# The opening of layer 1 in a two-layer hybrid block: a third weight group among the first products, token remainders on one engine

## The chip, the cores and the metric

The kernel runs on one core of a Trainium2 chip. The metric is device time in microseconds of one execution: the median of three runs is 1145.76 us, between 1138.57 and 1148.89. The profile is of one further execution.

## The reference

The reference is a two-layer block over 1024 latent tokens of width 1024 (plus 256 context tokens in layer 0). Layer 0 mixes Fourier channels and differential attention. Layer 1, where the change lies, is a gated short convolution:

```
h = rms_norm(x, g) * (1 + scale) + shift
bg, cg, xt, g = split(h @ odd_w_in, 4)          # 1024 x 1024 times 1024 x 4096
u = cg * xt
conv = sum(conv_w[t] * up[:, t:t+n] for t in range(3))
y = (bg * conv * silu(g)) @ odd_w_out
x = x + gate * y
```

## The kernel before, in words

Features lie on the 128 partitions, tokens along the free axis in two halves of 512. Every float32 product is made of three float32r matmuls: each operand is split in a rounded part and a remainder, and high times high, high times low and low times high are added up in PSUM. The helper `part` (lines 60 to 63) makes such a pair: ScalarE casts, and VectorE or GpSimd subtracts.

The products of layer 1 are further cut by a fast 2x2 block scheme. A **group** `g` is a pair of weight tiles `a`, `b` (512 KB each, `wload`, lines 1226 to 1237), and takes seven products `p` = 1 to 7 instead of eight. Groups 0 to 15 are the input projection (an even group makes `u`, the odd one after it the gate), 16 to 19 the output projection. A product is 12 matmuls of 128x512 (`quarters`, lines 639 to 648). Its moving operand `B[p]` comes from the tokens: `B[1]` and `B[2]` from half 0 alone; 5, 6, 7, 4 and 3 need half 1, whose RMS statistics are only known when layer 0's last projection is done. Its weight operand is made by `wop` (line 1239, with `wpart`, line 615): a cast on ScalarE and a remainder on VectorE or GpSimd, and for p = 5 sums of weight tiles on GpSimd (line 625).

A product adds into a PSUM bank by `"ZXZYXYXX"[p]`: p = 1, 6, 7, 4 into X, p = 5 and 3 into Y, p = 2 into Z. A group's Z bank is written by p = 2 alone and emptied by one VectorE addition (`finish1`, line 1282, `h0 += Z`). There are three X banks, two Y banks, **one Z bank**, and two more banks in the pool `pst`. With `later=True` (line 1259) a product returns its `finish1` as a function, and the caller places it later in the program.

The order of work in the opening (lines 1459 to 1487) is written out by hand, for TensorE, VectorE, ScalarE and GpSimd alike: each takes its instructions strictly in this order. Groups 0 and 1 run their products 1 and 2, then 5, 6, 7 and so on in pairs. Between the calls stand the token operands: `scaled` (row factors times scale, on VectorE, reading the PSUM bank `ps_r` that `rows_mid` filled), `t1` to `t4` (the differences), `hi` (a cast on ScalarE, line 1431) and `lo` (the remainder, line 1435, on VectorE `V` or GpSimd `G`). After the opening only TensorE's order is by hand, and the rest is placed by a scheduler when the program is built. When product 3 of a group has its weights (`wop`, p = 3), the tiles of group g + 2 are loaded. `finish1` for p = 3 of an even group also runs the convolution (`conv`, twelve short VectorE instructions, line 1315).

Of the kernel before, what the change touches and what calls it, by code (L numbers as in the profile page):

```python
# [8 lines left out]
F32 = mybir.dt.float32  # L9
F32R = mybir.dt.float32r  # L10
# [7 lines left out]
P = 128  # L18
# [4 lines left out]
KT = 8  # L23
# [14 lines left out]
def block_kernel(tc, A):  # L38
# [20 lines left out]
    def part(src, o, eng):  # L59

        nc.scalar.copy(out=o[:, 0, :], in_=src)  # L61
        eng.tensor_tensor(out=o[:, 1, :], in0=src, in1=f32(o[:, 0, :]), op=ALU.subtract)  # L62
        return o
# [1175 lines left out]
    def wop(g, p, eng=None):  # L1239
        pool = wpools[0]  # L1240
        wpools.append(wpools.pop(0))
        wops[g, p] = wpart(g, p, raws[g], done, lambda: w2.tile([P, NB], F32, name="s1", bufs=1),
                           lambda src, e: part(src, pool.tile([P, 2, NB], F32R, name="wop", bufs=4 if pool is wp else 2), e),
                           eng)
        if p == 3:
            wload(g + 2)

    banks = {}

    def product(g, p, mid=None, later=False):  # L1250
        bank = "ZXZYXYXX"[p]
        start = p in (1, 5, 2)
        if start:
            banks[g, bank] = acc.tile([P, NB], F32, name="ps" + bank, bufs={"X": 3, "Y": 2, "Z": 1}[bank])
        quarters(banks[g, bank], wops.pop((g, p)), [(x[:, 0, :], x[:, 1, :]) for x in B[p]], start, mid)
        fin = finish1 if g < 16 else finish2
        if later:
            return lambda: fin(g, p)
        fin(g, p)
# [4 lines left out]
    def finish1(g, p):  # L1264
        ct, gated = divmod(g, 2)
        X, Y_, Z = (banks.get((g, i)) for i in "XYZ")
        if p == 1:
            if g == 1:
                us[g] = [mp.tile([P, NB], F32, name="y", tag="x1ss", bufs=2) for _ in range(2)]
            elif gated:  # L1270
                us[g] = halves(xp.tile([P, T], F32, name="y", tag="x1", bufs=KT))
            else:
                i = ct % 2
                if ubuf[i] is None:
                    ubuf[i] = at0.tile([P, T], F32, name="u", tag="v0", bufs=1) if i == 0 else \
                        xp.tile([P, T], F32, name="u", tag="x1", bufs=KT)
                us[g] = halves(ubuf[i])
        h0, h1 = us[g]
        if p == 1:
            nc.scalar.copy(out=h0, in_=X)  # L1280
        elif p == 2:
            nc.vector.tensor_tensor(out=h0, in0=h0, in1=Z, op=ALU.add)
            if gated:
                nc.scalar.activation(out=h0, in_=h0, func=AF.Silu)
        elif p == 6:
            nc.scalar.copy(out=h1, in_=X)
        elif p == 7:
            c = part22[g] = mp.tile([P, NB], F32, name="c22", tag="xr", bufs=2)
            nc.scalar.copy(out=c, in_=X)  # L1289
            nc.vector.tensor_tensor(out=c, in0=c, in1=Y_, op=ALU.add)  # L1290
        elif p == 4:
            nc.vector.tensor_tensor(out=h0, in0=h0, in1=X, op=ALU.mult)
            if gated:
                nc.vector.tensor_mul(out=h0, in0=h0, in1=vv[:, 0:NB])
        elif p == 3:

            nc.vector.tensor_tensor(out=h1, in0=h1, in1=Y_, op=ALU.add)  # L1297
            if gated:
                nc.scalar.activation(out=h1, in_=h1, func=AF.Silu)
            nc.vector.tensor_tensor(out=h1, in0=h1, in1=part22.pop(g), op=ALU.mult)  # L1300
            if gated:
                nc.vector.tensor_mul(out=h1, in0=h1, in1=vv[:, NB:T])
                ysd.append(us[g])
            else:
                conv(ct, ubuf[ct % 2])
# [69 lines left out]
    for half in range(2):  # L1375
        y0(half)
        for f in range(KT):
            if half == 0 or f < KT - 1:
                w0next()
            if half == 1 and f == KT - 2:  # L1380
                wload(0)
                wload(1)
            if pend:
                ps = pend.pop(0)
            else:
                ps = proj_feat2(W[half * KT + f], half)
# [35 lines left out]
    def scaled(k):  # L1422
        t = x1[k][1]
        V.scalar_tensor_tensor(out=t, in0=t, scalar=scm(k), in1=late["r"], op0=ALU.mult, op1=ALU.mult)
# [4 lines left out]
    def hi(p, k):  # L1429
        o = B[p][k] = hB.tile([P, 2, NB], F32R, name=f"B{p}", bufs=4)  # L1430
        nc.scalar.copy(out=o[:, 0, :], in_=x1[k + 4 * (BSRC[p] // 2)][BSRC[p] % 2])

    def lo(p, k, eng):
        o = B[p][k]
        eng.tensor_tensor(out=o[:, 1, :], in0=x1[k + 4 * (BSRC[p] // 2)][BSRC[p] % 2], in1=f32(o[:, 0, :]),  # L1435
                          op=ALU.subtract)

    def shifted(k):
        scaled(k + 4)
        t = x1[k + 4][1]  # L1440
        nc.scalar.activation(out=t, in_=t, func=AF.Identity, bias=shm(k + 4))

    def t1(k):
        less(k, x1[k][0], x1[k][1], x1[k][0])
        hi(5, k)

    def t2(k):
        V.tensor_sub(out=x1[k][0], in0=x1[k + 4][1], in1=x1[k][0])
        hi(6, k)
# [5 lines left out]
    def t4(k):  # L1455
        V.tensor_sub(out=x1[k + 4][0], in0=x1[k + 4][0], in1=x1[k][0])
# [24 lines left out]
    t4(0), t4(1), lo(4, 0, V), lo(4, 1, G), t4(2), t4(3), lo(4, 2, V), lo(4, 3, V)
    product(0, 7)
    hi(3, 0), hi(3, 1), lo(3, 0, V), lo(3, 1, G), hi(3, 2), hi(3, 3), lo(3, 2, V), lo(3, 3, G)
    product(1, 7)
    wop(2, 1)
# [127 lines left out]
```

## Time and profile before

| what | us |
|---|---|
| median of three runs | 1145.76 |
| lowest, highest | 1138.57, 1148.89 |
| the profiled execution, its time | 1145.55 |
| its span, first to last instruction | 1143.8 |
| TensorE busy in the span | 1048.7 |
| VectorE, GpSimd, ScalarE busy | 757.5, 554.8, 492.7 |
| mean granted TensorE clock | 0.971 |

All times in rows count from the span's start. PE is TensorE, DVE VectorE, ACT ScalarE, POOL GpSimd, SP the engine whose queue issues the loads. A timeline row gives start, duration, engine, line, operation, output and inputs, shapes; an x2 means two instructions merged, and in brackets stand the idle time before it and what ended it. A windows row gives, for a stretch, each engine's busy time and count, the granted TensorE clock (PEclk), and what the DMA engines moved.

### The profile page before, as it was taken

How to read it: one execution, taken by the hardware profiler on the slowest of the kernel's cores; microseconds unless marked ns; L12 is line 12 of the kernel's file. 1: busy time of each engine (PE TensorE's matmuls, PEld its weight loads, DVE VectorE, ACT ScalarE, POOL GpSimd, SP SyncE). 2: the span in 40 equal slices, each digit the busy share in tenths (PEclk: the TensorE clock that was granted, in tenths of full speed). 3: DMA queues.
4: the chain of work that ended last, by engine and by line, in shares of the span. 5: the costliest groups of instructions: out<-in, count | busy, mean ns of one | idle time of the engine just before them, and what ended most of it. 6: DMA issues, size and time to landing. Idle time of an engine off the chain costs nothing.

```text
span 1143.8 us, 14185 instructions
## 1 busy us (share of the span) xinstructions
PE 1048.7 (92%) x5118; PEld 854.2 (75%) x5118; DVE 757.5 (66%) x1039; ACT 492.7 (43%) x888; POOL 554.8 (49%) x456
## 2 busy tenths in 40 slices
PE   4989898889898989999999998899999999998598
PEld 2657686668786869989988876578888888776486
DVE  4599932885859358888882376995546655578652
ACT  4463233221334357777773353543333333343320
POOL 1258656680466315766665445564344343432331
PEclk9999999999898999999999999999999999999899
DMA  9722995533220495551103642021111111111421
GB/s 341 294 93 83 270 299 179 181 90 108 74 97 10 133 259 140 132 131 60 47 28 120 203 156 92 21 71 56 56 56 56 56 41 70 56 55 65 159 80 64
DMA packets 61382, 131.12 MB, mean 115 GB/s; under 512 B 5249, under 2 KB 30209, under 8 KB 58113
## 3 DMA queue, kind: packets, MB, share of 16 engines
q1 hardware_dynamic: 60240, 125.64, 35.0%
q0 software_dynamic: 1072, 4.59, 1.1%
q8 instruction: 40, 0.66, 0.2%
q14 instruction: 30, 0.24, 0.1%
HBM read 105.57 MB, written 24.64 MB: 114 GB/s over the span
## 4 chain that ended last, share of the span: by engine, by line
PE 52%; DVE 17%; ACT 3%; DMA 2%; issue 2%; POOL 2%; SPq 0%; ACTq 0%; DVEq 0%; POOLq 0%
PE psX L646 6%; PE psX L648 6%; PE psX L647 6%; PE ps_av L1028 5%; PE psY L646 3%; PE psY L647 3%; PE psY L648 3%; PE S L978 2%; PE S L979 2%; PE ps_t L1018 2%; DVE nm L983 2%; PE ps_feat L1081 2%; PE ps_feat L1082 2%; PE ps_feat L1083 2%; DVE arena L62 2%
## 5 line engine op out<-in xcount | busy, mean ns | idle before, releaser
L61 ACT CAST wop<-wraw 128x512 fp32r<-128x512 f32 x152 | 93.6, 621 | 131.5 <-PE psY L648 30.0
L62 POOL TENSOR_TENSOR wop<-wraw,wop 128x512 fp32r<-128x512 f32 x72 | 99.4, 1383 | 77.4 <-ACT wop L61 77.3
L285 PE MATMUL ps_tok<-whi,hlo 128*128 128x512 f32 x288 | 116.9, 406 | 5.9 <-DVE hlo L394 5.9
L284 PE MATMUL ps_tok<-whi,hhi 128*128 128x512 f32 x288 | 119.9, 416 | 2.5 <-ACT hhi L390 2.5
L286 PE MATMUL ps_tok<-wlo,hhi 128*128 128x512 f32 x288 | 115.9, 402 | 0.3 <-POOL wlo L172 0.3
L983 DVE TENSOR_REDUCE nm<-S 128x1 f32<-128x1280 f32 x64 | 95.0, 1487 | 22.5 <-PE S L979 19.5
L646 PE MATMUL psX<-B,wop 128*128 128x512 f32 x240 | 97.1, 405 | 8.7 <-ACT c L1289 4.9
L994 ACT ACTIVATE p<-S,nm 128x1280 f32<-128x1280 f32 x64 | 85.3, 1332 | 45.0 <-DVE nm L983 41.3
L647 PE MATMUL psX<-B,wop 128*128 128x512 f32 x240 | 97.0, 404 | 1.5 <-POOL B L1435 1.1
L648 PE MATMUL psX<-B,wop 128*128 128x512 f32 x240 | 97.0, 404 | 0.5 <-POOL wop L62 0.5
L625 POOL TENSOR_TENSOR s<-wraw 128x512 f32<-128x512 f32 x20 | 27.7, 1383 | 122.3 <-DMA wraw<-in_wodd_dram 117.5
L625 POOL TENSOR_TENSOR wraw<-wraw 128x512 f32<-128x512 f32 x40 | 55.6, 1398 | 47.4 <-DVE wop L62 40.0
L62 DVE TENSOR_TENSOR wop<-wraw,wop 128x512 fp32r<-128x512 f32 x80 | 68.4, 857 | 13.3 <-ACT wop L61 13.0
L1028 PE MATMUL ps_av<-v,aT 128*128 128x128 f32 x640 | 76.8, 275 | 0.0
L1028 PEld LDWEIGHTS ps_av<-v,aT 128*128 128x128 f32 x640 | 74.2, 192 | 0.2
L1005 POOL TENSOR_TENSOR p<-p,cc 128x256 f32<-128x256 f32 x32 | 40.4, 1262 | 65.8 <-DVE cc L1002 45.2
L285 PEld LDWEIGHTS ps_tok<-whi,hlo 128*128 128x128 f32 x288 | 56.2, 195 | 20.6 <-DVE hlo L394 9.6
L284 PEld LDWEIGHTS ps_tok<-whi,hhi 128*128 128x128 f32 x288 | 56.0, 194 | 16.6 <-ACT hhi L390 3.8
L646 PE MATMUL psY<-B,wop 128*128 128x512 f32 x160 | 63.8, 399 | 4.8 <-DVE y L1297 3.0
L286 PEld LDWEIGHTS ps_tok<-wlo,hhi 128*128 128x128 f32 x288 | 56.1, 195 | 12.7 <-POOL wlo L172 0.7
L647 PE MATMUL psY<-B,wop 128*128 128x512 f32 x160 | 63.9, 399 | 0.3 <-POOL B L1435 0.3
L648 PE MATMUL psY<-B,wop 128*128 128x512 f32 x160 | 63.8, 399 | 0.0
(343 smaller groups left out, 2739.6 us busy)
## 6 DMA issues: line engine op xcount, KB each, us to landing
ada_raw<-in_ada_dram SPq DMA_DIRECT2D x24, 1024.0 KB, 7.4
wraw<-in_wodd_dram SPq DMA_DIRECT2D x32, 512.0 KB, 3.5
wraw<-in_wo_dram SPq DMA_DIRECT2D x24, 512.0 KB, 4.0
wraw<-in_wtok_dram SPq DMA_DIRECT2D x16, 512.0 KB, 5.1
arena<-kd SPq DMA_DIRECT2D x16, 320.0 KB, 9.1
kq<-kd SPq DMA_DIRECT2D x16, 320.0 KB, 9.8
xt<-in_xT_dram SPq DMA_DIRECT2D x16, 256.0 KB, 6.0
xr<-in_xT_dram SPq DMA_DIRECT2D x16, 256.0 KB, 4.0
```

Source lines behind the costliest of these rows:

```text
L61: nc.scalar.copy(out=o[:, 0, :], in_=src)
L62: eng.tensor_tensor(out=o[:, 1, :], in0=src, in1=f32(o[:, 0, :]), op=ALU.subtract)
L284: nc.tensor.matmul(ps, lhsT=hh, rhs=whi, start=k == 0, stop=False)
L285: nc.tensor.matmul(ps, lhsT=hl, rhs=whi, start=False, stop=False)
L286: nc.tensor.matmul(ps, lhsT=hh, rhs=wlo, start=False, stop=k == KT - 1)
L625: tt = lambda out, x, y, op: nc.gpsimd.tensor_tensor(out=out, in0=x, in1=y, op=op)
L646: nc.tensor.matmul(ps, lhsT=a, rhs=x[k][0], start=start and k == 0, stop=False, skip_group_check=not start)
L647: nc.tensor.matmul(ps, lhsT=a, rhs=x[k][1], start=False, stop=False, skip_group_check=not start)
L648: nc.tensor.matmul(ps, lhsT=b, rhs=x[k][0], start=False, stop=k == 3, skip_group_check=not start)
L983: nc.vector.tensor_reduce(out=nm, in_=S[m][:, :NKEY], op=ALU.max, axis=AX.X, negate=True)
L994: nc.scalar.activation(out=p, in_=S[m][:, :NKEY], func=AF.Exp, bias=tiles.pop((i, m, "nm")), accum_out=z)
L1028: nc.tensor.matmul(ps, lhsT=groups[i, k // 4][:, (k % 4) * P:(k % 4 + 1) * P], rhs=v[:, k * P:(k + 1) * P], start=k == 0, stop=k == NK - 1)
```

## The change

Three things are changed in the opening.

1. A third group joins it. `wload_early` loads the two weight tiles of group 2 a second time, in buffers of the tag `B3`, which the token operand `B[3]` takes over later; `wop_early` makes the operands of products 1, 2 and 5 of group 2 from them. The products (2,1) and (2,2) stand behind (1,2), and (2,5) behind (1,5), its Y bank out of the pool `pst`. Their `finish1` calls are put off (`fin2`). Later group 2's tiles come again by the usual `wload(2)`, and `wmix` redoes on GpSimd the sums that product 5 would have left in them.
2. The token remainders `lo` are all on VectorE (9 of 20 were on GpSimd), and the weight remainders of products 6, 7, 4 and 3 of groups 0 and 1 on GpSimd.
3. The order is new: `ps_r` is made in product (1,2) instead of (1,1); products 4 and 3 of group 1 and 6 of group 2 belong to the hand-written part; the multiplication of the gate of group 1 with `vv[:, 0:NB]` moves from p = 4 to p = 3.

```diff
+    def wload_early():
+        for i in range(2):
+            t = hB.tile([P, KT * P], F32, name="wraw", tag="B3", bufs=4)
+            nc.sync.dma_start(out=t, in_=A["wodd"][1, (1, 2)[i]])
+            early.append(t)
+    def wop_early(p):
+        pool = wpools[0]
+        wpools.append(wpools.pop(0))
+        wops[2, p] = wpart(2, p, early, set(), lambda: w2.tile([P, NB], F32, name="s1", bufs=1),
+                           lambda src, e: part(src, pool.tile([P, 2, NB], F32R, name="wop", bufs=4 if pool is wp else 2), e))
+    def wmix(g):
+        a, b = raws[g]
+        lo, hi = hsl
+        t = w2.tile([P, NB], F32, name="s1", bufs=1)
+        for o, x, y, op in ((t, b[:, lo], b[:, hi], ALU.add), (b[:, lo], b[:, lo], a[:, lo], ALU.subtract),
+                            (a[:, lo], t, a[:, lo], ALU.subtract), (a[:, hi], a[:, hi], a[:, lo], ALU.subtract)):
+            nc.gpsimd.tensor_tensor(out=o, in0=x, in1=y, op=op)
...
-            banks[g, bank] = acc.tile([P, NB], F32, name="ps" + bank, bufs={"X": 3, "Y": 2, "Z": 1}[bank])
+            banks[g, bank] = pst.tile([P, NB], F32, name="psY", tag="t", bufs=2) if (g, p) == (2, 5) else \
+                acc.tile([P, NB], F32, name="ps" + bank, bufs={"X": 3, "Y": 2, "Z": 1}[bank])
...
+    wload_early()
     product(0, 1)
-    wop(0, 6)
     product(0, 2, (2, stats_mid))
-    wop(1, 6, G)
-    product(1, 1, (2, rows_mid))
-    scaled(0), scaled(1), t1(0), scaled(2), t1(1), lo(5, 0, V), lo(5, 1, G), scaled(3), t1(2), t1(3), lo(5, 2, V)
-    lo(5, 3, G)
-    fin12 = product(1, 2, later=True)
-    product(0, 5)
+    wop_early(1)
+    product(1, 1)
+    wop_early(2)
+    fin12 = product(1, 2, (2, rows_mid), later=True)
+    scaled(0), scaled(1), t1(0), scaled(2), t1(1), lo(5, 0, V), lo(5, 1, V)
+    wop_early(5)
+    scaled(3), t1(2), t1(3), lo(5, 2, V), lo(5, 3, V)
+    fin2 = [product(2, p, later=True) for p in (1, 2)]
+    wop(0, 6, G)
+    product(0, 5)
+    shifted(0), shifted(1), t2(0), shifted(2), t2(1), lo(6, 0, V), lo(6, 1, V), shifted(3), t2(2), t2(3), lo(6, 2, V)
+    lo(6, 3, V)
+    wop(1, 6, G)
     product(1, 5)
...
+    product(2, 5)
+    fin12()
...
     product(0, 4)
+    wop(1, 3, G)
+    product(1, 4)
+    for f in fin2:
+        f()
+    wmix(2)
     product(0, 3)
+    wop(2, 6, V)
+    done.update(((2, 1), (2, 2), (2, 5)))
+    product(1, 3)
```

**TensorE, where the products without half-1 tokens end.** `arena_2059` and `arena_2060` are `B[1]` and `B[2]`; `B_6181` and `B_6185` are quarters of `B[5]`. Before, (1,2) is followed by (0,5):

```order
L648 MATMUL psZ<-arena_2060,wop 128x512
L646 MATMUL psY<-B_6181,wop 128x512 [waits Activation_49]
L647 MATMUL psY<-B_6181,wop 128x512 [waits DVE_49]
L648 MATMUL psY<-B_6181,wop 128x512
L646 MATMUL psY<-B_6185,wop 128x512 [waits Activation_49]
L647 MATMUL psY<-B_6185,wop 128x512 [waits Pool_49]
```

Now the last matmuls of (2,1), the first of (2,2), and further down the first of (0,5) (`B_6198` is now the first quarter of `B[5]`):

```order
L647 MATMUL psX<-arena_2059,wop 128x512
L648 MATMUL psX<-arena_2059,wop 128x512
L646 MATMUL psZ<-arena_2060,wop 128x512 [waits DVE_49,Activation_49]
L647 MATMUL psZ<-arena_2060,wop 128x512
L648 MATMUL psZ<-arena_2060,wop 128x512
L646 MATMUL psY<-B_6198,wop 128x512 [waits Activation_49]
```

The first matmul of (2,2) waits for ScalarE, which casts its weights, and for VectorE. What VectorE has to reach is its addition of (1,2)'s Z bank, since (2,2) takes the same bank.

**VectorE, where that addition stands.** Before, after the differences and the VectorE share of the remainders of `B[6]` (`B_6254` is one):

```order
L1448 TENSOR_TENSOR x_5567<-x_5727,x_5567 128x512 [waits Activation_49,Pool_49]
L1435 TENSOR_TENSOR B_6254<-x_5527,B_6254 128x512 [waits Activation_49]
L1282 TENSOR_TENSOR y<-y,psZ 128x512 [waits PE_49]
L1427 SCALAR_TENSOR_TENSOR x_5498<-x_5498,shift_90,x_5607 128x512
L1427 SCALAR_TENSOR_TENSOR x_5512<-x_5512,shift_90,x_5647 128x512
```

Now (the line numbers of the changed file are higher; L1478 was L1448, L1465 was L1435, L1308 was L1282):

```order
L1478 TENSOR_TENSOR x_5567<-x_5727,x_5567 128x512 [waits Activation_49]
L1465 TENSOR_TENSOR B_6281<-x_5527,B_6281 128x512 [waits Activation_49]
L1465 TENSOR_TENSOR B_6284<-x_5567,B_6284 128x512 [waits Activation_49]
L1308 TENSOR_TENSOR y<-y,psZ 128x512 [waits PE_49]
L1457 SCALAR_TENSOR_TENSOR x_5498<-x_5498,shift_90,x_5607 128x512
```

The addition has kept its place behind all of `B[5]` and `B[6]`: 20 instructions stand between the first `scaled` and it before, and 25 now, the five more being four remainders and one weight remainder of (2,5).

**VectorE, around the convolution of group 0.** Before, the weight remainder of (2,6) (the L62 row) stands after the fifth of the convolution's twelve instructions (L1315):

```order
L1315 SCALAR_TENSOR_TENSOR vv<-u,small,vv 128x254 [waits DVE_49]
L1315 SCALAR_TENSOR_TENSOR vv<-u,small,vv 128x255 [waits Activation_49]
L62 TENSOR_TENSOR wop<-wraw,wop 128x512 [waits Activation_49]
L1292 TENSOR_TENSOR y<-y,psX 128x512 [waits PE_49]
L1315 SCALAR_TENSOR_TENSOR vv<-u,small,vv 128x255 [waits DVE_49]
```

Now the end of the convolution (L1343, as L1315 is now called), and behind it the weight remainder of (2,6):

```order
L1343 SCALAR_TENSOR_TENSOR vv<-u,small,vv 128x254 [waits DVE_49]
L1343 SCALAR_TENSOR_TENSOR vv<-u,small,vv 128x2
L1343 SCALAR_TENSOR_TENSOR vv<-u,small,vv 128x2 [waits DVE_49] x2
L1343 SCALAR_TENSOR_TENSOR vv<-u,small,vv 128x2
L62 TENSOR_TENSOR wop<-wraw,wop 128x512 [waits DMAHW3_49,Activation_49]
L1323 TENSOR_TENSOR y<-y,psY 128x512 [waits PE_49]
```

The remainder of (2,6) is now behind the whole convolution; (2,6) itself is the product right behind (1,3) on TensorE.

More of the change, by code (lines that the diff above doesn't have):

```diff
@@ L1246, in wop @@
             wload(g + 2)
+    def wload_early():
[15 more added lines that the diff above has]
+            nc.gpsimd.tensor_tensor(out=o, in0=x, in1=y, op=op)
+    early = []
     banks = {}
@@ L1266, in finish1 @@
         X, Y_, Z = (banks.get((g, i)) for i in "XYZ")
+        if p == 5:
+            return
         if p == 1:
@@ L1292, in finish1 @@
             nc.vector.tensor_tensor(out=h0, in0=h0, in1=X, op=ALU.mult)
-            if gated:
+            if gated and g > 1:
                 nc.vector.tensor_mul(out=h0, in0=h0, in1=vv[:, 0:NB])
@@ L1301, in finish1 @@
             if gated:
+                if g == 1:
+                    nc.vector.tensor_mul(out=h0, in0=h0, in1=vv[:, 0:NB])
                 nc.vector.tensor_mul(out=h1, in0=h1, in1=vv[:, NB:T])
@@ L1362, in finish2 @@
             take(Y_, 1, (f, 1))
-    order = [(0, 1), (0, 2), (1, 1), (1, 2), (0, 5), (1, 5), (0, 6), (1, 6), (0, 7), (1, 7), (0, 4), (0, 3)]
-    for g in range(2, 14):
+    order = [(0, 1), (0, 2), (1, 1), (1, 2), (2, 1), (2, 2), (0, 5), (1, 5), (2, 5), (0, 6), (1, 6), (0, 7), (1, 7),
+             (0, 4), (1, 4), (0, 3), (1, 3), (2, 6), (2, 7)]
+    NMAN = 17
+    for g in range(3, 14):
         order += [(g, 1), (g - 1, 4), (g, 5), (g - 1, 3), (g, 6), (g, 2), (g, 7)]
@@ L1387, in block_kernel @@
             if half == 1 and f == KT - 1:
-                for q in order[:5]:
+                for q in (*order[:4], (0, 5)):
                     wop(*q)
@@ L1459, in block_kernel @@
     nc.scalar.activation(out=l2[:, 0:1], in_=ones[:, 0:1], func=AF.Silu)
+    wload_early()
     product(0, 1)
-    wop(0, 6)
     product(0, 2, (2, stats_mid))
-    wop(1, 6, G)
-    product(1, 1, (2, rows_mid))
-    scaled(0), scaled(1), t1(0), scaled(2), t1(1), lo(5, 0, V), lo(5, 1, G), scaled(3), t1(2), t1(3), lo(5, 2, V)
-    lo(5, 3, G)
-    fin12 = product(1, 2, later=True)
-    product(0, 5)
+    wop_early(1)
[10 more added lines that the diff above has]
+    lo(6, 3, V)
+    wop(1, 6, G)
     product(1, 5)
-    shifted(0), shifted(1), t2(0), shifted(2), t2(1), lo(6, 0, V), lo(6, 1, G), shifted(3), t2(2), t2(3), lo(6, 2, V)
-    lo(6, 3, G)
+    product(2, 5)
+    fin12()
     wop(0, 7, G)
-    fin12()
-    t3(0), t3(1), lo(7, 0, V), lo(7, 1, G)
+    t3(0), t3(1), lo(7, 0, V), t3(2), lo(7, 1, V), t3(3), lo(7, 2, V), lo(7, 3, V)
     product(0, 6)
-    t3(2), t3(3), lo(7, 2, V), lo(7, 3, G)
     wop(1, 7, G)
     product(1, 6)
+    t4(0), t4(1), lo(4, 0, V), t4(2), lo(4, 1, V), t4(3), lo(4, 2, V), lo(4, 3, V)
     wop(0, 4, G)
+    product(0, 7)
+    wop(1, 4, G)
+    product(1, 7)
+    hi(3, 0), hi(3, 1), lo(3, 0, V), hi(3, 2), lo(3, 1, V), hi(3, 3), lo(3, 2, V), lo(3, 3, V)
     wop(0, 3, G)
[L1481 to L1485, printed above, removed]
-    product(0, 4)
+    product(0, 4)
+    wop(1, 3, G)
[3 more added lines that the diff above has]
+    wmix(2)
     product(0, 3)
+    wop(2, 6, V)
+    done.update(((2, 1), (2, 2), (2, 5)))
+    product(1, 3)
     man.__exit__(None, None, None)
@@ L1494, in block_kernel @@
              (16, 1): [(7, 3, 4), (4, 0, 2)], (16, 5): [(4, 2, 4)], (17, 1): [(3, 0, 4)]}
-    wn = 13
+    wn = NMAN + 1
     for n, (g, p) in enumerate(order):
-        if n < 12:
+        if n < NMAN:
             continue
```

## The prediction

> **What bounds the kernel now.** I read the page's busy line first, then stretches of the windows view around the opening, then TensorE's waits there.
>
> ```profile
> PE 1048.7 (92%) x5118; PEld 854.2 (75%) x5118; DVE 757.5 (66%) x1039; ACT 492.7 (43%) x888; POOL 554.8 (49%) x456
> ```
> ```profile
> 709.90:716.70 6.80, 5.85 (x12) 3.95 (x13) 4.92 (x8) 1.18 (x3) 0.34 (x1) 0.50 0.01 2
> 716.70:744.00 27.30, 22.03 (x84) 14.69 (x83) 26.68 (x29) 16.43 (x29) 16.91 (x11) 1.00 0.09 26
> 744.00:747.40 3.40, 3.40 (x9) 2.63 (x8) 3.40 (x4) 3.00 (x6) 2.89 (x2) 0.50 0.25 102
> 774.80:992.70 217.90, 217.90 (x935) 175.06 (x934) 122.10 (x192) 79.60 (x134) 92.95 (x68) 1.00 0.17 56
> ```
>
> From 774.8 to 992.7 us TensorE is never idle and the clock is at 1.00: 217.90 busy of 217.90. So nothing else sets the pace there, and what the opening gains or loses is carried to the end one for one. Between 716.7 and 744.0 VectorE is busy for 26.68 of 27.30 us and TensorE is not: there VectorE is the bound. The stalls themselves:
>
> ```profile
> PE ps_r L228 <- DVE dg L220: 3.5, 1, 3.5
> PE psX L646 <- ACT c L1289: 2.5, 1, 2.5
> PE psX L646 <- ACT u L1286: 2.5, 1, 2.5
> PE psX L647 <- POOL B L1435: 1.1, 2, 0.8
> ```
> ```profile
> 698.43 0.40 PE L646 MATMUL psX<-arena,wop 128*128 128x512 f32 x1
> ...
> 702.63 0.28 PE L209 MATMUL ps_ss<-ones,x1ss 128*128 128x1 f32 x2
> ...
> 704.34 0.48 PE L646 MATMUL psZ<-arena,wop 128*128 128x512 f32 x1
> ...
> 706.99 0.39 PE L648 MATMUL psX<-arena,wop 128*128 128x512 f32 x1
> 710.85 2.08 PE L228 MATMUL ps_r<-dg,ones 128*128 128x512 f32 x2 [3.47 <-DVE dg L220]
> 711.93 1.42 PE L646 MATMUL psX<-arena,wop 128*128 128x512 f32 x1
> ...
> 744.01 0.63 PE L648 MATMUL psX<-B,wop 128*128 128x512 f32 x1
> ...
> 816.56 0.40 PE L646 MATMUL psX<-B,wop 128*128 128x512 f32 x1
> ```
>
> At full clock a matmul takes 217.90 / 935 = 0.233 us, so a product of twelve 2.80; at clock 0.50, from the row at 744.00, 3.40 / 8 = 0.43. The first product starts at 698.43 and the 35th at 816.56: 118.1 us for 34 products (95.2) and the token sums (702.63 to 704.34, 1.7). The opening therefore **loses 21.2 us now**: the wait for `ps_r`, its own 2.08, three stretches at half clock (a full one of 3.4 us costs 3.4 x (1 - 0.233/0.43) = 1.55), two ScalarE waits of 2.5, and small waits for remainders. That is all the change can win.
>
> **The change part by part.** Matmuls are neither added nor removed. I rebuild the same ledger of 34 products.
>
> *The early loads.* Two tiles of 512 KB more.
>
> ```profile
> wraw<-in_wodd_dram SPq DMA_DIRECT2D x32, 512.0 KB, 3.5
> 693.81 7.21 SPq L1175 DMA_DIRECT2D x1d<-x  x2
> ```
>
> SP's queue issues them behind the first of these two writes, from about 694.2, the second when the last projection has left its buffer; 3.5 us each, so they land by about 701, and the first is used at 705. Behind them only the last `x1d` write is passed, which is read at the very end. Cost 0; if they came 3 us late, (2,1) still would not wait, because of what follows.
>
> *The first wait for the Z bank.* (1,2) may start once VectorE has added (0,2)'s bank, an instruction that stands behind `dg`.
>
> ```profile
> 706.00 1.29 POOL L625 TENSOR_TENSOR wraw<-wraw 128x512 f32<-128x512 f32 x1
> 707.76 0.15 DVE L216 TENSOR_SCALAR rs<-ps_ss 128x4 f32<-128x4 f32 x1
> 707.99 1.02 POOL L218 TENSOR_TENSOR rs<-rs,mhalf 128x4 f32<-128x4 f32 x1 [0.70 <-DVE rs L216]
> 709.04 1.75 DVE L220 TENSOR_TENSOR dg<-cst,rs 128x512 f32<-128x512 f32 x1 [1.13 <-POOL rs L218]
> 710.71 0.67 DVE L1282 TENSOR_TENSOR u<-u,psZ 128x512 f32<-128x512 f32 x1
> ```
>
> The weight remainder that kept VectorE's `rs` until 707.8 is gone, so GpSimd's `rs` follows its mixing at 707.3, `dg` comes at 708.3, and the addition ends at 710.7 if `dg` again takes 1.75, at 709.7 if it takes 0.7. TensorE has finished (0,1), (0,2), the token sums and (1,1) at 698.4 + 8.4 + 1.7 = 708.5: it loses **2.1** (bounds 1.0 and 2.1). Then `ps_r` in mid-product costs **1.0**, half of 2.08 as no long idle precedes it (up to 2.1). `ps_r` is ready at 713.2, not earlier than now.
>
> *The second wait for the Z bank.* (1,2) ends at 714.5 and (2,1) at 717.3. (2,2) needs the only Z bank, which VectorE empties by an instruction behind all of `B[5]` and `B[6]`.
>
> ```profile
> 712.96 1.41 DVE L1424 SCALAR_TENSOR_TENSOR x<-x,sc,ps_r 128x512 f32<-128x512 f32 x2 [1.57 <-PE ps_r L228]
> 727.73 0.68 DVE L1282 TENSOR_TENSOR y<-y,psZ 128x512 f32<-128x512 f32 x1
> ```
> ```profile
> L1435 DVE TENSOR_TENSOR B<-x,B x11: 678/693/1772, 716.7 to 746.3; 128x512 fp32r<-128x512 f32 x11
> 738.79 3.46 DVE L1456 TENSOR_TENSOR x<-x,x 128x512 f32<-128x512 f32 x2
> 736.58 5.12 POOL L62 TENSOR_TENSOR wop<-wraw,wop 128x512 fp32r<-128x512 f32 x3
> ```
>
> Now 20 instructions take from 712.96 to 727.73, 14.8 us. The change has 25, the five more at some 0.6 each in a dense row (3.0), from 713.2: the addition runs at about 731.0 less 0.4, as GpSimd now crosses this stretch three times and not four, and ends at 731.3. TensorE stands still from 717.3 to 731.3: **14.0**. The 738.79 rows show what a crossing is: two VectorE subtractions take 3.46 us, not 1.3, while GpSimd works through the row at 736.58. So the lower bound is 25 x 0.65 with no crossing and an early `dg` (11), the upper one three more crossings (16). `B[5]` and `B[6]` are all there by then, so the small waits of now vanish in this one.
>
> *Half clock after it.* Now a 3.5 us wait was followed by two windows of 0.50 (709.90 to 716.70), a 2.5 us wait by one. For a 14 us wait I take 1.5 windows, **2.3** (1.5 to 3.1).
>
> The Trainium skill, TensorE: Matmul & The Clock Gate, Part 1, says that one busy window of about 3.4 us brings the full clock back. The rows at 709.90 show two; by the page alone both half-clock terms here would be 1.55, and the time 1158.1.
>
> *Products from then on.* From 731.3 run (2,2), (0,5), (1,5), (2,5), (0,6), (1,6), (0,7), (1,7), (0,4), (1,4), (0,3), (1,3): 33.6 us, and 2.3 for the clock, to 767.2. VectorE's remaining 12 differences and remainders of `B[7]`, `B[4]`, `B[3]`, at 0.6 to 1.3, have 8.4 us to get ahead of (0,7), since ScalarE lets `B[7]` start only when (1,5) is done; I see no wait, and the pairing hides the copies that cost 2.5 now. This is the gain of the change, and it cannot be more than the 21.2.
>
> *(2,6) behind the convolution.* Its weight remainder stands behind the whole convolution of group 0, which starts when (0,3) is done.
>
> ```profile
> 754.34 0.68 DVE L1300 TENSOR_TENSOR u<-u,c 128x512 f32<-128x512 f32 x1
> ...
> 758.21 0.69 DVE L62 TENSOR_TENSOR wop<-wraw,wop 128x512 fp32r<-128x512 f32 x1
> ...
> 767.62 0.69 DVE L1294 TENSOR_TENSOR y<-y,vv 128x512 f32<-128x512 f32 x1
> ```
>
> Now (2,6)'s remainder comes at 758.21, 3.9 us after `u*c`, and the convolution ends at 767.6, 13.3 us after it, with GpSimd crossing. In the change (0,3) ends at 764.4, `u*c` starts at 765.1, and 13.3 + 0.7 later, at 779.1, the remainder is there. TensorE has finished (1,3) at 767.2 and can run two matmuls of (2,6): 11.4, and one more for GpSimd, which is denser here (the repeated sums of `wmix`, the weights of groups 2 and 3): **12.4**. Upper bound 15. Lower bound: the reloaded tile itself. It is issued when (0,3)'s weight remainder is done, about 760, lands 3.5 us later, is mixed by three GpSimd sums of 1.3 to 1.7 and cast (0.6) by 769; with the remainder right behind the cast, (2,6) would wait 3. I take the row of the convolution, since the order is fixed.
>
> Half clock again, **2.0** (0 to 3.1), and (2,7), now directly behind (2,6) on the same X bank, waits for ScalarE's copy, **1.0** (0.5 to 1.2; the same wait now was 2.5 with ScalarE late).
>
> Sum: 2.1 + 1.0 + 14.0 + 2.3 + 12.4 + 2.0 + 1.0 = 34.8, against 21.2: **13.6 us more**. On the profiled execution's 1145.55 (span 1143.8 and 1.75 around it) this is 1159.2; its time is within 0.2 of the median. All lower ends together (1.0, 1.0, 11, 1.5, 3, 0, 0.5: 18) give 1142.4, all upper ends (2.1, 2.1, 16, 3.1, 15, 3.1, 1.2: 42.6) 1167.
>
> **The rivals.** *The third group fills the hole (not slower).* If (2,2) does not wait for VectorE, TensorE has 5.6 us more work while `B[5]` is made, the losses shrink to `ps_r`, one window and some 2 us of remainders, about 5, and the time is 1145.6 - 16 = 1129.5. For it: the rows of now show just such holes, and later TensorE runs dry nowhere. Against it: one Z bank, and the addition's place behind 25 VectorE instructions. It decides if the addition comes before 717.
>
> *Only the first stall comes.* The convolution on VectorE runs without crossings: its instructions of 256 elements take 0.4 to 0.5 alone, so the remainder comes with the cast at 769, and (2,6) waits 3 without a half-clock window. 34.8 - 9.4 - 2.0 = 23.4, 2.2 more than now: 1147.8. Against it: in the row at 754.94 GpSimd's sums stretched just these instructions, and GpSimd has more to do there.
>
> ```profile
> 754.94 3.35 DVE L1315 SCALAR_TENSOR_TENSOR vv<-u,small,vv 128x256 f32<-128x256 f32 x5
> ```
>
> *The pipeline stays late.* After (2,6) the weights of group 3 and 4 are behind: SP reloads group 2 first, one group's tiles later than now, and each product from (3,1) to (4,1) waits a little more, some 6 us: 1165. Against it: TensorE's 12.4 us at rest let the other engines catch up.
>
> **How the numbers follow.** A measurement of this kernel tells about 1% (11.5 us) from no change, so slower begins at 1157.2. Forecast, both stalls, 1154 to 1164: 0.65, of which 0.52 lie over 1157.2. Only the first stall: 0.18, all within 1%. The hole filled: 0.07, 0.06 of it faster. Late pipeline: 0.10, slower. So faster 0.06, same 0.01 + 0.13 + 0.18 = 0.32, slower 0.62. The time is the forecast's, 1159.2. The range, 1147 to 1167, takes in the second rival and the upper bounds, and leaves out the filled hole and a little on each side.
>
> **What would show it.** In the changed profile: a wait of some 14 us of TensorE before psZ (L646), ended by VectorE's addition `y<-y,psZ` near 731; windows of 0.50 behind it; no more waits for the copies `c` and `u` of groups 0 and 1; a second wait of some 12 us before `psX<-B`, ended by a weight remainder on VectorE behind the convolution; then TensorE at rest nowhere up to the output groups. Wrong is the forecast if the first wait is under 8 us, or if the second ends with ScalarE's cast.

## The result, and the profile after

The changed kernel takes 1158.75 us in the median of four runs (1156.12 to 1160.26); the kernel before, run four times beside it, takes 1146.76 in the median (1138.57 to 1148.89). The ratio on record is **1.0125, with a 95% interval of 1.0097 to 1.0152** (the two medians alone give 1.0105): slower by a little over 1%, as forecast, and 0.5 us from the forecast's 1159.2. How much of this closeness is luck stands further down. The profiled execution took 1158.7 us, its span is 1156.9.

First the waits of TensorE from 698 us to 830 us, the columns being the total, the number of waits and the longest:

```profile
PE psZ L646 <- DVE y L1308: 13.6, 1, 13.6
PE psX L648 <- DVE wop L62: 9.2, 1, 9.2
PE psX L646 <- ACT wop L61: 2.1, 1, 2.1
PE psZ L646 <- DVE u L1308: 1.9, 1, 1.9
```

The list of before had many waits, of 3.5 us and less. Now two waits make 22.8 of 27.7 us, both for VectorE (behind these rows stand only 0.7 and 0.2). One stands before `psZ` and is ended by the addition `y<-y,psZ` (L1308 in the changed file), the other before the third matmul of a product into `psX` and is ended by a weight remainder (L62).

Next the timeline of TensorE: the matmuls behind a wait, and some product starts.

```profile
706.17 0.40 PE L646 MATMUL psX<-arena,wop 128*128 128x512 f32 x1
...
711.07 0.50 PE L646 MATMUL psZ<-arena,wop 128*128 128x512 f32 x1 [1.93 <-DVE u L1308]
...
714.81 0.39 PE L646 MATMUL psX<-arena,wop 128*128 128x512 f32 x1
...
731.40 0.77 PE L646 MATMUL psZ<-arena,wop 128*128 128x512 f32 x1 [13.63 <-DVE y L1308]
...
735.74 0.39 PE L646 MATMUL psY<-B,wop 128*128 128x512 f32 x1
...
764.21 0.40 PE L646 MATMUL psY<-B,wop 128*128 128x512 f32 x1
...
769.25 0.50 PE L646 MATMUL psX<-B,wop 128*128 128x512 f32 x1 [2.07 <-ACT wop L61]
769.58 0.40 PE L647 MATMUL psX<-B,wop 128*128 128x512 f32 x1
779.19 0.80 PE L648 MATMUL psX<-B,wop 128*128 128x512 f32 x1 [9.21 <-DVE wop L62]
...
783.92 0.50 PE L646 MATMUL psX<-B,wop 128*128 128x512 f32 x1 [0.68 <-ACT u L1312]
```

From such rows the ledger of 34 products (the list of what each of them lost) is made as in the prediction: each product takes 2.80 us at full clock, and what it takes longer is lost. The first product starts at 698.79 and the 35th at 828.83, which is 130.04; less 95.2 for the products and 1.7 for the token sums, **33.1 us are lost, against 21.2 before**.

| term of the prediction | forecast | measured | from which rows |
|---|---|---|---|
| wait for the Z bank before (1,2) | 2.1 | 2.10 | 706.17 to 711.07, less 2.80 |
| `ps_r` inside (1,2) | 1.0 | 0.94 | 711.07 to 714.81, less 2.80 |
| wait for the Z bank before (2,2) | 14.0 | 13.79 | 714.81 to 731.40, less 2.80 |
| half clock behind it | 2.3 | 1.54 | 731.40 to 735.74, less 2.80 |
| (2,6) and its weight | 12.4 | 11.7 | 2.24 up to 769.25, 9.4 at 779.19, 0.1 between |
| half clock behind it | 2.0 | 1.56 | ten matmuls, 779.19 to 783.08, less 2.33 |
| (2,7), copy on ScalarE | 1.0 | 0.84 | 783.08 to 783.92 |
| not forecast | 0 | 0.6 | 0.47 at a weight remainder of (1,4), 0.1 at (3,1) |
| sum | 34.8 | 33.1 | |

The rest of the difference lies outside: layer 1 starts 0.4 later (698.79 against 698.43), and the last 42 products take 144.25 us, not 143.23. 11.9 + 0.4 + 1.0 = 13.3, and the spans differ by 13.1. Between the opening and these last products TensorE is never idle:

```profile
792.00:1005.00 213.00, 213.00 (x915) 171.09 (x913) 117.70 (x190) 77.38 (x130) 88.88 (x65) 1.00 0.17 57
```

The VectorE rows that set the two long waits, with start and duration:

```profile
713.62 1.41 DVE L1454 SCALAR_TENSOR_TENSOR x<-x,sc,ps_r 128x512 f32<-128x512 f32 x2 [0.92 <-PE ps_r L228]
...
730.57 0.68 DVE L1308 TENSOR_TENSOR y<-y,psZ 128x512 f32<-128x512 f32 x1
...
765.13 0.69 DVE L1326 TENSOR_TENSOR u<-u,c 128x512 f32<-128x512 f32 x1
765.74 7.15 DVE L1343 SCALAR_TENSOR_TENSOR vv<-u,small,vv 128x256 f32<-128x256 f32 x5
772.82 1.75 DVE L62 TENSOR_TENSOR wop<-wraw,wop 128x512 fp32r<-128x512 f32 x1
774.49 4.05 DVE L1343 SCALAR_TENSOR_TENSOR vv<-u,small,vv 128x255 f32<-128x255 f32 x7
778.45 0.69 DVE L62 TENSOR_TENSOR wop<-wraw,wop 128x512 fp32r<-128x512 f32 x1
```

The addition ends at 731.25, 17.6 us after the first `scaled` began, with 25 instructions ahead of it that take 16.95 us together, 0.68 each (the forecast: 731.3). The remainder of (2,6) ends at 779.14, behind the twelve instructions of the convolution and one weight remainder that the scheduler put between them (the forecast: 779.1). Five convolution instructions take 7.15 us while GpSimd works through its sums. The other seven take 4.05: two more of 1.48 each, then, with GpSimd's last sum over at 777.08, one of 0.48 and four on two elements each.

### The profile page after: what moved, and what is told of

It is laid out like the page before. It is cut to its first block, busy times and chain, and to the rows that moved or that the text cites. A ratio compares the mean times of both kernels' runs of the same rounds, so it can differ in the third digit from the quotient of the medians.

```text
span 1156.9 us, 14194 instructions
## 1 busy us (share of the span) xinstructions
PE 1041.9 (90%) x5118; PEld 851.3 (74%) x5118; DVE 750.9 (65%) x1046; ACT 492.0 (43%) x888; POOL 548.1 (47%) x452
## 4 chain that ended last, share of the span: by engine, by line
PE 57%; DVE 14%; ACT 3%; issue 3%; DMA 2%; POOL 1%; SPq 0%; ACTq 0%; DVEq 0%; POOLq 0%
PE psX L648 6%; PE psX L646 6%; PE psX L647 6%; PE ps_av L1028 5%; PE psY L646 3%; PE psY L647 3%; PE psY L648 3%; PE ps_feat L1081 3%; PE ps_feat L1082 3%; PE ps_feat L1083 3%; PE S L978 2%; PE S L979 2%; PE ps_t L1018 2%; DVE nm L983 2%; PE psZ L646 2%
## 5 line engine op out<-in xcount | busy, mean ns | idle before, releaser
L62 POOL TENSOR_TENSOR wop<-wraw,wop 128x512 fp32r<-128x512 f32 x74 | 100.8, 1366 | 115.6 <-ACT wop L61 115.4
L648 PE MATMUL psX<-B,wop 128*128 128x512 f32 x240 | 95.8, 399 | 9.4 <-DVE wop L62 9.2
L646 PE MATMUL psX<-B,wop 128*128 128x512 f32 x240 | 96.0, 400 | 6.4 <-ACT c L1315 2.7
L647 PE MATMUL psX<-B,wop 128*128 128x512 f32 x240 | 95.3, 397 | 0.0
L62 DVE TENSOR_TENSOR wop<-wraw,wop 128x512 fp32r<-128x512 f32 x78 | 64.4, 827 | 13.5 <-ACT wop L61 13.3
```

Source lines behind the costliest of these rows:

```text
L646: nc.tensor.matmul(ps, lhsT=a, rhs=x[k][0], start=start and k == 0, stop=False, skip_group_check=not start)
L647: nc.tensor.matmul(ps, lhsT=a, rhs=x[k][1], start=False, stop=False, skip_group_check=not start)
L648: nc.tensor.matmul(ps, lhsT=b, rhs=x[k][0], start=False, stop=k == 3, skip_group_check=not start)
```

## The experiments

Each kernel is run beside the kernel before on the same chip, and the ratio is to that. "Lost" is the ledger of 34 products of its profile, made from the start of the first product and of the 35th. It leaves out layer 0 and the end, and so tells smaller differences apart than the time does. But it comes from one profile of each kernel. Many of its terms repeat to 0.1 (the wait before (2,2) costs 13.79 in the change and 13.80 in kernel 3), others do not: before (1,2), with nothing altered up to there, kernel 7 loses 1.6 where the change and kernels 1 to 4 lose 2.1. So differences of the ledger under 1 us are not read as gains here.

The expectations of kernels 1 to 4 are in us, on the scale of the first measurement (1158.8 for the change, 1146.8 for the kernel before). In the session of these runs the kernel before took 1142.7, so a ratio times 1146.8 is what has to be held against them.

| kernel | 1st, 35th product | lost | ratio to before, 95% interval |
|---|---|---|---|
| before | 698.43, 816.56 | 21.2 | 1 |
| the change | 698.79, 828.83 | 33.1 | 1.0125 (1.0097 to 1.0152) |
| 1 addition early | 694.55, 814.72 | 23.3 | 1.0051 (1.0026 to 1.0076) |
| 2 own bank | 692.41, 811.93 | 22.6 | 1.0013 (0.9995 to 1.0032) |
| 3 weight before convolution | 697.25, 820.63 | 26.5 | 1.0077 (1.0052 to 1.0102) |
| 4 both moved | 700.82, 814.62 | 16.9 | 0.9998 (0.9980 to 1.0016) |
| 5 before, all on VectorE | 694.99, 812.14 | 20.3 | 0.9996 (0.9979 to 1.0013) |
| 6 both moved, shared | 695.34, 816.10 | 23.9 | 1.0026 (1.0007 to 1.0044) |
| 7 addition between | 699.79, 822.92 | 26.2 | 1.0072 (1.0049 to 1.0095) |
| 8 four moves | 695.33, 808.86 | 16.6 | 0.9951 (0.9931 to 0.9970) |
| 9 before, no third group | 697.17, 813.07 | 19.0 | 0.9977 (0.9963 to 0.9991) |
| 10 three moves | 699.61, 812.53 | 16.0 | 0.9964 (0.9950 to 0.9979) |

**1. The addition early.** Theory A is that of the prediction: the places of two VectorE instructions make the two waits. Theory B is that VectorE's load as such does.

```diff
-    scaled(0), scaled(1), t1(0), scaled(2), t1(1), lo(5, 0, V), lo(5, 1, V)
+    scaled(0), scaled(1)
+    fin12()
+    t1(0), scaled(2), t1(1), lo(5, 0, V), lo(5, 1, V)
...
     product(2, 5)
-    fin12()
```

> The changed kernel, with the addition of the Z bank of (1,2) placed behind the second `scaled` instead of behind all of `B[5]` and `B[6]`; nothing else moves by hand. Theory A (place of the addition): VectorE makes it near 716, so (2,2) runs on from (2,1) at 717.6, and the wait of 13.6 us with its half-clock window (1.5) is gone. VectorE's row is as long as it was, so some of the 15 is given back where TensorE catches up with the remainders of B[7], and at (2,6): 1146 to 1150, against 1158.8 for the changed kernel. Theory B (VectorE's load): the row of 25 instructions itself is what TensorE needs, the addition is only its last member; then TensorE waits about as long for B[5] or B[6], the gain is under 3 us: 1156 to 1159.

Measured: 1.0051, 23.3 lost. The last matmul of (2,1) starts at 713.16 and the first of (2,2) at 713.39: the wait of 13.6 is gone, and its half clock. What TensorE waits for later is this (its timeline):

```profile
734.26 0.79 PE L646 MATMUL psX<-B,wop 128*128 128x512 f32 x1 [3.32 <-ACT u L1312]
...
765.24 0.79 PE L648 MATMUL psX<-B,wop 128*128 128x512 f32 x1 [9.21 <-DVE wop L62]
```

5.1 of the 15.3 us come back at (0,7), which now waits 3.3 for ScalarE's copy of (0,6) and runs on at half clock; (2,6) waits as long as ever. One instruction's place was worth 10 us of the ledger, so theory A has the cause and B falls. By the ratio A's range of time was missed (1.0051 is 1152.6 us); the ledger's 9.9 us would lie in it (1148.9).

**2. A bank of its own for (2,2).** VectorE's order is untouched.

```diff
-            banks[g, bank] = pst.tile([P, NB], F32, name="psY", tag="t", bufs=2) if (g, p) == (2, 5) else \
+            banks[g, bank] = pst.tile([P, NB], F32, name="psY", tag="t", bufs=2) if (g, p) in ((2, 2), (2, 5)) else \
```

> The changed kernel, with (2,2) adding into a bank of its own, out of the pool pst (as (2,5) does), and VectorE's order untouched: the addition of (1,2) stays behind B[5] and B[6]. Theory A (bank and place): (2,2) has nothing to wait for but its weights and starts at 717.6; (2,5) takes the bank that ps_r leaves and may wait some 1 us for the last `scaled` near 728; 1146 to 1150. Theory B (VectorE's load): 1156 to 1159, since VectorE does exactly the same work in the same order.

Measured: 1.0013, 22.6 lost. The wait before (2,2) is gone though the addition is as late as before; (2,5), which takes the bank that `ps_r` held, shows the small wait that was expected (1.69). A row of VectorE:

```profile
724.22 0.68 DVE L1308 TENSOR_TENSOR y<-y,psZ 128x512 f32<-128x512 f32 x1
```

The addition comes at 724.22, 31.8 us after the first product of this run (31.8 in the changed kernel too), and nobody waits for it. So it was the bank, and nothing that VectorE computes, that held (2,2). The ratio is 1148.3 us on the scale of the expectation, in theory A's range.

**3. The weight of (2,6) ahead of the convolution.**

```diff
     wmix(2)
+    wop(2, 6, V)
     product(0, 3)
-    wop(2, 6, V)
```

> The changed kernel, with the weight operand of (2,6) made before product (0,3) in the program, so that its remainder on VectorE stands ahead of the convolution of group 0. Theory A (place of the remainder): the cast ends near 769 and the remainder follows at once, (2,6) runs through, the wait of 9.2 and its half-clock window (1.5) are gone. The convolution starts some 4 us later, so up to 5 us come back at a later product of groups 1 to 3 that needs its banks or its weights: 1148 to 1155. Theory C (the repeated load and its mixing make (2,6) late, the order hardly): the wait stays at 6 us or more, 1155 to 1159.

Measured: 1.0077, 26.5 lost. TensorE's waits in the stretch, from its list:

```profile
PE psX L646 <- ACT y L1312: 2.9, 1, 2.9
...
PE psX L648 <- DVE wop L62: 0.7, 1, 0.7
```

The 9.2 are 0.7. Of the repeated load and its mixing only the wait for the cast is left (1.6), so theory C falls: the place behind the convolution was the cause. As expected some of it returns: with the convolution later, a copy of group 3 on ScalarE stands behind the next convolution's and costs 2.9. In time (1.0077, or 1155.6 us) the result lies at the edge of both theories' ranges; it is the waits that decide.

**4. Both moves.** The edits of kernels 1 and 3 together.

> The changed kernel with both moves: the addition early and the weight of (2,6) ahead of the convolution. Theory A: the two waits are separate places, the gains add but for what VectorE's row gives back: 1137 to 1144, which is faster than the kernel before (1146.8) and shows that the third group as such wins. Theory B (VectorE's load is the bound, whatever the order): not under 1147.

Measured: 0.9998, 16.9 lost. The gains add in the ledger (9.9 from the one, 6.7 from the other, 16.2 from both), and theory B's limit is passed there. The time does not show it: the ratio is 1146.6 us, just under B's limit of 1147 and short of A's 1137 to 1144; 4.3 us less lost than before should give 0.996, and the interval ends at 0.998. So this kernel is as fast as the one before, and no faster as far as the time shows; why the ledger's 4.3 us are missing in it stays open. One thing that blurs it lies outside the ledger. Over the twelve profiles layer 1 starts anywhere from 692.4 (kernel 2) to 700.8 (this one), though up to 690 us all four engines run the same instructions in the same order in all of them. The kernel before, one build, spread over 1137.2 to 1146.2 in the 26 runs beside kernels 1 to 4, so execution alone can make a spread of that size; that it makes this one is not shown.

**5. The second part of the change alone,** in the kernel before; so for all nine remainders that stood on `G` (of the weights only the remainder of (1,3) stays where the scheduler had it).

```diff
-    wop(0, 6)
+    wop(0, 6, G)
...
-    lo(5, 3, G)
+    lo(5, 3, V)
```

> The kernel before with the second part of the change alone: all token remainders on VectorE, and the weight remainder of (0,6) on GpSimd; no third group, the order otherwise as it was. Theory A (places of two waits): this part is only the smaller contributor, VectorE gets 9 instructions of some 0.6 more and one less, GpSimd stops crossing it with 1.6 us ones; the ledger of 34 products goes from 21.2 lost to between 20 and 25, the ratio to before is 0.999 to 1.003. Theory B (VectorE's load is what cost the time): most of the 12 us of the change should come from here, a ratio over 1.006.

Measured: 0.9996, 20.3 lost: no difference. Nine more instructions on VectorE cost nothing that can be seen here, so VectorE's load is not what made the change slow. It does set the pace of what is left at (0,7), as kernels 1 and 8 show.

**6. Both moves, with the nine remainders back on GpSimd;** so in each of the rows for 5, 6, 7, 4 and 3.

```diff
-    scaled(3), t1(2), t1(3), lo(5, 2, V), lo(5, 3, V)
+    scaled(3), t1(2), t1(3), lo(5, 2, V), lo(5, 3, G)
```

> The kernel with both moves (ratio 0.9998 to the kernel before, 16.9 us lost over 34 products), with the 9 token remainders given back to GpSimd as before. Theory A': a remainder costs GpSimd 1.3 to 1.7 us and VectorE 0.6, and the two cross each other, so sharing is the slower way in a dense row: TensorE waits 3 to 4 us for B[5] near (0,5), 20 to 25 lost, ratio 1.003 to 1.007. Theory B (VectorE's load): sharing relieves VectorE, under 15 lost, ratio under 0.998.

Measured: 1.0026 (just under the range of A'), 23.9 lost; A' holds in size but its reason was not the main one. TensorE waits 3.3 us at (0,5); ahead of that stand a row of VectorE and two of GpSimd:

```profile
717.28 1.23 DVE L62 TENSOR_TENSOR wop<-s,wop 128x512 fp32r<-128x512 f32 x1 [3.36 <-ACT wop L61]
```
```profile
714.05 1.28 POOL L1465 TENSOR_TENSOR B<-x,B 128x512 fp32r<-128x512 f32 x1 [8.74 <-ACT B L1461]
715.29 1.30 POOL L625 TENSOR_TENSOR s<-wraw 128x512 f32<-128x512 f32 x1
```

GpSimd stood idle 8.7 us for the cast of its token remainder, with the weight sums of (2,5) queued behind it; their cast came late, and VectorE stood idle 3.36 for that, ahead of half of `B[5]`. It is again an order: work that was ready, behind work that was not. With the third group the second part of the change is worth 7 us of the ledger, without it (kernel 5) 1 at most.

**7. The addition between `B[5]` and `B[6]`.**

```diff
     scaled(3), t1(2), t1(3), lo(5, 2, V), lo(5, 3, V)
+    fin12()
...
     product(2, 5)
-    fin12()
```

> The changed kernel with the addition of (1,2)'s bank at a third place, behind B[5] and ahead of B[6]; the weight of (2,6) stays where the change has it. Theory A (place of the addition): 13 of the 25 VectorE instructions stand ahead of it, so it ends near 722 to 723 (counted with the first product at 698.8), and TensorE's wait before (2,2) is 5 to 6 us instead of 13.6. What TensorE has in reserve there it doesn't need to wait for later at (0,7), so in all no worse than with the earliest place: 21 to 24 lost, ratio 1.002 to 1.006. Theory B (load): wait still over 9, ratio over 1.008.

Measured: 1.0072, 26.2 lost. The wait is the 5.3 us that the place foretells:

```profile
723.65 0.77 PE L646 MATMUL psZ<-arena,wop 128*128 128x512 f32 x1 [5.32 <-DVE y L1308]
```

Three places of one instruction give waits of 0, 5.3 and 13.6. The sum was missed (26.2 lost for 21 to 24, 1.0072 for at most 1.006): 7.9 us are paid here (5.5 and 2.45 of half clock), and only 5.1 are saved at (0,7), so this place is worse than the early one in the ledger; half clock was the size that I had too small.

**8. Four moves.** Two more are added to those of kernel 4: `dg` behind the addition of (0,2), and `wop(0, 3, G)` ahead of `B[3]`.

```diff
     def stats_mid():
-        late["dg"] = stats1(1)
+        late["ss"] = token_sums(ssq[1], NB)
+    def dg_late():
+        late["dg"] = rms_diag(late["ss"], NB, mp, ("xr", 2))
...
     product(0, 2, (2, stats_mid))
+    dg_late()
...
+    wop(0, 3, G)
     hi(3, 0), hi(3, 1), lo(3, 0, V), hi(3, 2), lo(3, 1, V), hi(3, 3), lo(3, 2, V), lo(3, 3, V)
-    wop(0, 3, G)
```

> Both moves and two more: dg is made behind the addition of (0,2)'s bank, not ahead of it, and the weight operand of (0,3), which starts the reload of group 2's tiles, stands ahead of B[3] and not behind it. Theory A: the wait of 1.9 before (1,2) is gone, and the wait for the cast of (2,6) (2.1) shrinks to under 1 as the tiles land some 2 us earlier; part of it comes back at (0,7), where VectorE sets the pace: 13.5 to 16 lost, ratio 0.996 to 0.999. Theory B (VectorE's row sets the time of everything behind it): both gains are given back in full, 16.5 to 17.5 lost.

Measured: 0.9951, 16.6 lost: faster than both kernels, by half a per cent against the one before. The time is below even theory A's range, while the ledger is theory B's, by the 0.6 us that it lies above A's: the 1.9 before (1,2) is gone, and comes back at (0,5) and from (2,6) on. The largest single loss that is left, 5.2 us with its half clock, is (0,7); TensorE's row first, then ScalarE's:

```profile
733.89 0.50 PE L646 MATMUL psX<-B,wop 128*128 128x512 f32 x1 [3.33 <-ACT u L1312]
```
```profile
732.73 0.62 ACT L1464 CAST B<-x 128x512 fp32r<-128x512 f32 x1 [0.65 <-DVE x L1460]
733.26 0.58 ACT L1312 COPY u<-psX 128x512 f32<-128x512 f32 x1
```

The copy that frees an X bank stands behind four casts of `B[7]`, each of which waits for VectorE, and VectorE is busy 7.15 of 7.23 us there. So (0,7) waits for VectorE's row once more.

**9. The moves without the third group.** Kernel 5, with `stats_mid` and `dg_late` as in kernel 8, and:

```diff
     product(0, 2, (2, stats_mid))
+    dg_late()
     wop(1, 6, G)
-    product(1, 1, (2, rows_mid))
+    product(1, 1)
+    fin12 = product(1, 2, (2, rows_mid), later=True)
...
-    fin12 = product(1, 2, later=True)
```

> No third group: the kernel before with all token remainders on VectorE, ps_r made in (1,2) and not in (1,1), and dg made behind the addition of (0,2)'s bank. Theory A (the third group, once its two waits are gone, is what fills the hole): without it TensorE meets the unfinished quarters of B[5] and B[6] right behind (1,2); the 3.5 us it no longer waits for ps_r comes back there, 19 to 22 lost, ratio 0.998 to 1.002, clearly above the four moves with the third group (0.9951). Theory D (the gain of the four moves comes from the order of dg and ps_r and the third group is worth nothing): under 17.5 lost, ratio 0.993 to 0.997.

Measured: 0.9977, 19.0 lost. In the ledger it is theory A's lowest number, in the ratio it lies just past A's edge and short of D's; neither theory's in full. The rows behind (1,2):

```profile
714.27 0.50 PE L646 MATMUL psY<-B,wop 128*128 128x512 f32 x1 [1.41 <-ACT B L1434]
715.55 0.50 PE L647 MATMUL psY<-B,wop 128*128 128x512 f32 x1 [0.78 <-DVE B L1438]
```

Without the third group TensorE runs into the unfinished `B[5]`, as expected. The order, with the remainders on VectorE, gives 2.2 us of the ledger over the kernel before. The third group, with its waits removed and with whatever else of the change's order comes with it, gives about 3 more (19.0 to 16.0 in kernel 10); in time the two kernels' intervals overlap, so this last step rests on one profile each.

**10. Three moves.** Kernel 8 less this:

```diff
+    wop(0, 3, G)
     hi(3, 0), hi(3, 1), lo(3, 0, V), hi(3, 2), lo(3, 1, V), hi(3, 3), lo(3, 2, V), lo(3, 3, V)
-    wop(0, 3, G)
```

> The changed kernel with the early addition, the weight of (2,6) ahead of the convolution, and dg behind the addition of (0,2)'s bank; the weight of (0,3) stays where the change has it. The ledger of 34 products lies between those of the two moves (16.9) and the four (16.6), so the time should lie between them too: ratio 0.995 to 0.999. If it comes out near 1.000, like the two moves, the reload of the tiles is what made the four moves faster than the ledger says; if near 0.995, the two moves' 0.9998 was high by scatter outside layer 1's opening.

Measured: 0.9964, 16.0 lost. It lies between 4 and 8 in time, nearer to 8, so the reload of the tiles is not what made kernel 8 fast, and the ratio of kernel 4 was probably high by something outside the opening (argued, not shown: the intervals of 4 and 10 overlap). In the ledger, where it was expected between the two (16.6 to 16.9), it lies below both, by less than the ledger can tell.

## Why the prediction was right, point by point

- **TensorE without reserve (shown).** From 792 to 1005 us TensorE is busy for 213.00 of 213.00 us, as it was from 774.8 to 992.7 before, and each product from the 21st to the 97th starts at the same distance from its fellow in the kernel before (11.91 us later, counted from the first product). What the opening loses is carried to the end.
- **The Z bank (shown, kernels 1, 2 and 7).** The place of one instruction behind 25 others is the price: 13.79 measured, 14.0 forecast. The three crossings by GpSimd that the forecast counted in did not come (GpSimd begins one instruction in that stretch, at 722.22): none of the 25 takes over 0.75 us, and at 0.68 us each they filled the time.
- **The weight of (2,6) (shown, kernel 3).** 11.7 against 12.4. I put all of it on the remainder; 2.2 were already a wait for the cast of the reloaded tile, which the forecast had counted only as its lower bound.
- **The gain in between (right in size, the reason only in part).** From 735.74 to 764.21 ten products take 28.47 us, 0.47 over 28.0, where copies and remainders cost some 9 us before. The prediction gave this to the pairing and to the lead that the other engines get. Kernel 1 divides the two: once the long wait is gone, 5.1 us come back at (0,7). So about half of this gain was paid for by the wait of 13.6 us, in which the other engines got ahead.
- **The half clock (too large, both terms).** 1.54 and 1.56 for 2.3 and 2.0. The page of the Trainium skill had it better here: TensorE: Matmul & The Clock Gate, Part 1, says that one busy window of about 3.4 us brings the full clock back, which makes an estimate of 1.55 with the rows' 0.233 and 0.43 us for a matmul. (By that estimate the forecast's time would have been 1158.0; the prediction's 1158.1 is a slip.) It is no fixed price, though: kernel 7 paid 2.45. The last section shows why, and why the kernel before had two windows.
- **Not foreseen.** The last 42 products take 1.0 us longer. The place is a product behind the 12 us wait near the end that both kernels have: it loses 2.45 instead of 1.45, and 2.2 to 2.5 in all ten experiments. So the odd one is the profile of the kernel before, and this 1.0 us is not the change's doing as far as the runs show.
- **The time (0.5 us off, in part luck).** The ledger grew by 11.9 us where 13.6 were forecast: the half clock (1.2 too much) and (2,6) (0.7) are most of that. A later start of layer 1 (0.4) and the 1.0 us at the end, neither of them forecast and neither shown to come from the change, fill most of the gap. And single runs of the kernel before differ by 10 us (1138.57 to 1148.89), so the nearness of 1158.75 to 1159.2 proves less than the ledger's terms do.
- **The rivals.** The filled hole (1129.5) asked that the addition come before 717. Kernels 1 and 4 bring that about, and even in kernel 4 16.9 us stay lost, not 5: TensorE then gets ahead of VectorE's `B[7]` (5.1 at (0,7)), and the rival also left out 4.9 at (2,6) and (2,7), 3.1 at a product of group 3 and the 2.1 before (1,2). Only the first stall: that asked for a convolution without crossings. It did not come, since seven of its instructions took 1.36 to 1.52 us where the one after GpSimd's last sum took 0.48. The forecast's argument was weaker than the outcome: in its own row at 754.94 only the first of the five was slow (1.52, the others 0.48). The late pipeline did not come: after (2,7) TensorE waits nowhere up to the output groups.

## What to carry to other kernels

Before you give an idle engine more work, list what each added piece waits for besides its operands: an accumulator bank is freed by an instruction of another engine, and the number of instructions ahead of that one, times their duration, is the price (forecast 14.0 here, measured 13.8, and 10 us of the ledger back from moving that one line). When a bank is scarce, empty it as soon as it is full, and put what the next product needs ahead of a long row that is needed only later, such as the convolution here. Then look where the time comes back: in kernels 1 and 3 TensorE then waited for the next late engine (5.1 us of 15.3 in kernel 1).

## What the runs showed of the hardware that I had not expected

**The half clock is not a fixed price.** The windows view, cut at the clock's own steps of 3.4 us (after the time and length stand TensorE, its weight loads, VectorE, ScalarE and GpSimd; the granted clock is third from the end). The changed kernel:

```profile
717.40:720.85 3.45, 0.37 (x2) 0.00 (x0) 3.36 (x6) 1.29 (x3) 0.00 (x0) 1.00 0.00 0
720.85:724.25 3.40, 0.00 (x0) 0.00 (x0) 3.25 (x6) 2.46 (x5) 1.27 (x1) 0.52 0.01 2
...
731.10:734.50 3.40, 3.10 (x7) 2.48 (x8) 1.48 (x3) 0.00 (x0) 0.00 (x0) 0.50 0.00 0
734.50:737.90 3.40, 3.40 (x16) 2.74 (x15) 0.00 (x0) 0.00 (x0) 0.00 (x0) 0.98 0.00 0
```

The kernel before, and then kernel 7:

```profile
709.90:713.30 3.40, 2.45 (x4) 1.33 (x5) 1.83 (x3) 0.00 (x0) 0.34 (x1) 0.50 0.02 5
713.30:716.70 3.40, 3.40 (x10) 2.63 (x9) 3.10 (x6) 1.18 (x3) 0.00 (x0) 0.50 0.00 0
716.70:720.10 3.40, 3.40 (x16) 2.74 (x15) 3.37 (x5) 1.42 (x3) 1.29 (x1) 1.00 0.00 0
```
```profile
721.85:725.25 3.40, 1.60 (x4) 1.35 (x5) 2.97 (x5) 2.04 (x5) 0.50 (x1) 0.53 0.01 2
725.25:728.65 3.40, 3.40 (x10) 2.66 (x9) 3.22 (x5) 2.51 (x5) 0.78 (x1) 0.50 0.00 0
728.65:732.05 3.40, 3.40 (x16) 2.71 (x15) 3.13 (x5) 1.88 (x4) 0.00 (x0) 0.96 0.00 0
```

One nearly idle window (0.37 busy) brings the clock to 0.5, and a busy one brings it back, but a window in which the work resumes late does not count: 3.10 of 3.40 busy was enough, 2.45 and 1.60 were not. So the price is the time from the resumption to the end of the first window that is busy enough, times 1 - 0.233/0.43, or 0.46: 3.1 us of it in the changed kernel, 5.0 in kernel 7, which gives 1.4 and 2.3 (measured 1.54 and 2.45). The shorter wait drew more half clock behind it than the longer one, because it ended 1.6 us into a window (kernel 7's runs from 722.06 to 725.47) and the other 0.2 us into one (731.20 to 734.61). In all of these one window that was busy enough brought the clock back. The Trainium skill, TensorE: Matmul & The Clock Gate, Part 1, has the same rule of one busy window; the rows add how busy that is. In layer 1 of the twelve profiles the least busy window that brought the clock back had TensorE busy for 2.91 of 3.41 us (kernel 1), and the busiest that did not 2.85 (kernel 9):

```profile
764.74:768.15 3.41, 2.91 (x7) 2.33 (x8) 3.41 (x7) 0.63 (x1) 0.00 (x0) 0.50 0.19 53
```
```profile
715.94:719.35 3.41, 2.85 (x7) 1.46 (x6) 3.39 (x6) 1.24 (x2) 0.00 (x0) 0.50 0.00 0
```

In layer 0, with its other matmuls, busy time alone does not separate them: 2.93 was not enough in kernel 3 (299.39 to 302.80), and 2.70 was in the changed kernel (222.60 to 226.00).
